# A hybrid block's planner gets new durations and handovers, and the attention copy is queued behind its scores

## The chip, the cores and the metric

The kernel runs on one core of one Trainium2 chip. The metric is the device time of one execution in microseconds (us), and lower is better. Times of before are the median of three runs.

## The reference

Two layers, each a mixer with three branches followed by a convolutional feed-forward network, on 16 meta tokens and 256 tokens of width 1024. All is float32. Cut to what matters:

```python
for li in range(DEPTH):                                   # DEPTH = 2
    h = h + mixer(rms_norm(h, norm_mix_g[li]), ...)
    h = h + conv_ffn(rms_norm(h, norm_ffn_g[li]), ...)
h = rms_norm(h, norm_final_g)
return h[:, PAD:]

def mixer(hn, ...):
    proj = hn @ w_in                                      # 1024 x 13312, split in 12
    o_ret = retention(rq, rk, rv, rg)                     # 4 heads, chunks of 128, decayed state
    o_hg = hgrn2(hq, hf, hi, hg, lb)                      # 8 heads, a gated scan: a = sum q k exp(cumsum gap)
    o_da = diff_attention(dq, dk, dv, lam, subln_g)       # 8 heads, two softmaxes subtracted, causal
    y = sum(sigmoid(gate_n) * (branch_n @ w_branch_n))
    return y @ w_out

def conv_ffn(hn, ...):
    u = hn @ w_ffn_in                                     # 1024 x 5632
    c = conv_b + sum(conv_w[j] * shifted(u, j) for j in range(3))
    return (silu(gate) * val) @ w_ffn_out                 # 2816 x 1024
```

## The kernel before

Activations are kept transposed, features on the partitions and the 272 tokens (16 meta + 256) in the free dimension; in the second layer most stages work on 258 or 256 tokens. TensorE has no full float32 product at this speed, so each factor is split into a high and a low part and each tile of 128 x 128 weights is multiplied three times: high by high (L923), low activations by high weights (L924), high activations by low weights (L925). In the profile these are the groups `main<-xh,whi`, `main<-xl,whi` and `main<-xh,wlo`: the "main matmuls". A triple of them is one step of the plan, recorded by `products` (L900 on).

All weights are one stream of some 400 chunks of 128 x 1024 (eight tiles). SyncE's queue loads a chunk into `wraw` (three buffers), ScalarE rounds it into `whi` (an activation that copies), VectorE subtracts and leaves `wlo`; `whi` and `wlo` have four buffers each. Twenty-four main matmuls use a chunk, in about 3 us.

Between the main matmuls stand the "side groups" of the three branches. Their names in the profile:

- `ms` is the matmul with ones that makes a norm's mean square, from `sum`; `rstd` follows on ScalarE, then the products `y<-h,rstd` on GpSimd.
- HGRN2 works in blocks: a group of small matmuls recorded by one helper (L1132: `lev`, `pm`, `far`), then VectorE's masked copies (`near<-masks,lev`, `am<-masks,pm`: a copy under a mask of bytes) and products (`hq`, `hf` with `tot`), ScalarE's copies into `at`, then `px` (whose copy is `ax`), `ht`, and the outputs `ho`. There are four such blocks, two in each layer. Each begins near 97, 197, 746 and 837 us.
- Retention: scores `s`, decayed on VectorE into `wts`, outputs `ro`, then a norm whose sums are reduced over the partitions by GpSimd (`hr<-sum`).
- Attention works on pairs of heads in `da_heads` (L1387 on): one step `scores` of the plan makes both heads' scores (`ds`), VectorE and ScalarE make the softmaxes in `two_a` and `two_b`, `wt` transposes them, ScalarE copies them into a buffer with the tag `wts` (the variable `a1`, "a head's weight buffer"; two of them), and `do` multiplies by the values. The first 16 columns of `a1`, for the meta tokens, are copied by GpSimd (`wts<-am`) from weights made earlier.

What sets the order of all this is written out by a planner. Every operation goes through `_Engine.__getattr__` (L601 is its recording line, which is why so many groups have that line), which gives it a duration by a formula of its size, and `_Plan.add`, which finds the operations on which it depends. Then `_Plan.order` runs a list scheduler over the whole program: at each step it takes the engine that can start first, and on it the operation with the smallest start, then the smallest key. The key is a due time (`plan.key`, `clock`); with the durations it decides the order. Constants in it:

- CROSS: the time from the end of an operation to the start of one on another engine that depends on it.
- FREE: the time from the last use of a buffer until another may take it.
- SWITCH: a change of ScalarE's activation table, 1.3.
- SHARED: the share by which a VectorE operation is taken to last longer while GpSimd is busy.
- PIECE, MANY, BEGIN: a group of 200 or more TensorE instructions may only begin in certain windows of each 256 instructions.

The plan fixes no time on the chip: it gives each engine its list of instructions, and the waits there are the semaphores of the data. The engines are recorded with the formulas `fixed + each * n`, n being the elements of a partition:

```python
act = _Engine(plan, nc.scalar, "act", 0.094, 0.833e-3)
dve = _Engine(plan, nc.vector, "dve", 0.068, 1.042e-3)
pool = _Engine(plan, nc.gpsimd, "pool", 0.04, 0.85e-3)
```

`plan.queue(first, last)` makes `first` wait for `last` in the plan; `plan.hold` lists buffers that an operation takes when it starts. PSUM is used as two buffers "main" of two banks, two "bank" and two "acc".

## Time and profile before

| | |
|---|---|
| median of 3 runs | 1285.73 us (1285.28 to 1286.61) |
| the profiled execution | 1286.2 us |
| its span | 1284.4 us |
| mean granted clock of TensorE | 0.999 |
| HBM read, written | 216.19 MB, 1.05 MB |
| DMA, mean | 175 GB/s |

The span is what the profiler records from the first to the last instruction; the profiled execution's own time is 1.8 us longer. A busy time of 99% for TensorE says that records lie end to end, and not that each is as short as it could be. The two layers lie one after the other: the matmul `ms` of the norm that opens the second starts at 665 us. A window of the profile is read as the busy time of each engine in a stretch; where TensorE has less than the length of the window, something was waited for there, and the timeline shows what.

The order of the instructions of both kernels is known without a run, as each program is built. TensorE has 10171 instructions in both, VectorE 1635, GpSimd 183, SyncE 445, and they are the same ones. ScalarE has six more table loads after the change (33 in place of 27). The orders differ from the first norm on; the first 99 main matmuls and the last stage have the same order. The largest moves on TensorE: the fourth HGRN2 block from 837.2 to 851.5 (in TensorE time, main matmuls and groups laid end to end with the lengths of before), the retention groups behind it some 9 us later, attention groups of the first layer 2 to 10 us earlier.

### The profile page before, as it was taken

The numbers are of one execution on the slowest core, as the hardware profiler recorded it, in microseconds if no ns is written. First come the engines' busy times: TensorE is split into PE (matmuls) and PEld (weight loads), VectorE is DVE, ScalarE is ACT, GpSimd is POOL, SyncE is SP. The second block draws the span as 40 slices with busy tenths as digits, with TensorE's granted clock in tenths as the row PEclk, the third lists the DMA queues.
The fourth block names the chain that finished last, engine by engine and source line by source line (L and its number), as shares of the span: only waits on it lengthen the run. The fifth ranks groups of instructions, "written<-read, shape, count | busy, mean of one in ns | idle before, by whom it ended". The sixth has DMA issues, their size and how long they took to land.

```text
span 1284.4 us, 26932 instructions
## 1 busy us (share of the span) xinstructions
PE 1275.5 (99%) x10825; PEld 1253.6 (98%) x10825; DVE 973.0 (76%) x1657; ACT 855.6 (67%) x1460; POOL 165.9 (13%) x174
## 2 busy tenths in 40 slices
PE   9999999999999999999999999999999999999998
PEld 9999999999999999999999999999999999999986
DVE  7686787698685789886565858886987867998753
ACT  6766575856776568776456754858567765787743
POOL 4001101132122020000020011012131210300000
PEclk9999999999999999999999999999999999999999
DMA  8655575544745555555555556745447466566663
GB/s 281 193 165 170 175 192 177 150 148 133 211 134 165 185 163 187 175 177 176 173 177 185 164 178 177 206 163 164 148 136 210 137 201 191 166 192 199 197 188 107
DMA packets 86093, 225.28 MB, mean 175 GB/s; under 512 B 32208, under 2 KB 32336, under 8 KB 85968
## 3 DMA queue, kind: packets, MB, share of 16 engines
q1 hardware_dynamic: 85680, 223.03, 56.9%
q8 instruction: 85, 1.39, 0.5%
q10 hardware_dynamic: 288, 0.52, 0.1%
q14 instruction: 40, 0.33, 0.1%
HBM read 216.19 MB, written 1.05 MB: 169 GB/s over the span
## 4 chain that ended last, share of the span: by engine, by line
PE 98%; DVE 1%; ACT 1%; DMA 0%; issue 0%; SPq 0%
PE main L925 29%; PE main L923 29%; PE main L924 28%; PE fo L1538 2%; PE fo L1540 2%; PE fo L1539 2%; PE ds L1409 1%; PE ro L601 1%; PE do L601 1%; PE ho L601 1%; PE lev L1132 1%; PE wt L601 0%; PE s L601 0%; DMA h<-in_h 0%; PE far L1132 0%; PE px L601 0%
## 5 line engine op out<-in xcount | busy, mean ns | idle before, releaser
L923 PE MATMUL main<-xh,whi 128*128 128x272 f32 (+1 forms) x2368 | 685.6, 290 | 0.2 <-ACT whi L601 0.2
L925 PE MATMUL main<-xh,wlo 128*128 128x272 f32 (+1 forms) x2368 | 679.6, 287 | 0.5 <-DVE wlo L601 0.4
L924 PE MATMUL main<-xl,whi 128*128 128x272 f32 (+1 forms) x2368 | 670.1, 283 | 0.0
L601 DVE TENSOR_TENSOR wlo<-wraw,whi 128x1024 fp32r<-128x1024 f32 (+1 forms) x408 | 507.1, 1249 | 205.6 <-ACT whi L601 203.3
L601 ACT ACTIVATE whi<-wraw 128x1024 fp32r<-128x1024 f32 (+1 forms) x408 | 426.2, 1049 | 211.8 <-PE main L924 118.7
L924 PEld LDWEIGHTS main<-xl,whi 128*128 128x128 f32 x2368 | 449.3, 190 | 0.3
L923 PEld LDWEIGHTS main<-xh,whi 128*128 128x128 f32 x2368 | 445.2, 188 | 1.7 <-ACT whi L601 0.4
L925 PEld LDWEIGHTS main<-xh,wlo 128*128 128x128 f32 x2368 | 444.5, 188 | 1.4 <-DVE wlo L601 1.4
L601 POOL PARTITION_ALL_REDUCE hr<-hsq x36 | 75.5, 2119 | 147.6 <-ACT hsq L601 147.5
L601 POOL TENSOR_TENSOR y<-h,rstd 128x272 f32<-128x272 f32 x32 | 38.5, 1235 | 319.6 <-ACT rstd L601 319.6
L601 DVE SCALAR_TENSOR_TENSOR two_b<-u,small,two_b 128x256 f32<-128x256 f32 (+2 forms) x176 | 78.4, 486 | 0.6 <-ACT two_b L601 0.2
L925 PE MATMUL main<-ghi,wlo 128*128 128x272 f32 x176 | 51.0, 290 | 0.0
L923 PE MATMUL main<-ghi,whi 128*128 128x272 f32 x176 | 50.8, 288 | 0.0
L924 PE MATMUL main<-glo,whi 128*128 128x272 f32 x176 | 50.1, 285 | 0.0
L601 ACT ACTIVATE two_b<-u,small 128x272 f32<-128x272 f32 (+1 forms) x88 | 49.4, 599 | 1.1 <-DVE glo L601 0.7
L601 ACT ACTIVATE u<-main 128x544 f32<-128x544 f32 (+1 forms) x40 | 24.5, 613 | 34.1 <-PE main L925 34.0
L923 PE MATMUL main<-b0hi,whi 128*128 128x272 f32 (+1 forms) x128 | 37.5, 293 | 0.0
L923 PE MATMUL main<-b1hi,whi 128*128 128x272 f32 (+1 forms) x128 | 37.3, 292 | 0.0
L925 PE MATMUL main<-yhi,wlo 128*128 128x272 f32 (+1 forms) x128 | 36.5, 285 | 0.0
L925 PE MATMUL main<-b2hi,wlo 128*128 128x272 f32 (+1 forms) x128 | 36.5, 285 | 0.0
L925 PE MATMUL main<-b1hi,wlo 128*128 128x272 f32 (+1 forms) x128 | 36.5, 285 | 0.0
L925 PE MATMUL main<-b0hi,wlo 128*128 128x272 f32 (+1 forms) x128 | 36.5, 285 | 0.0
(262 smaller groups left out, 1919.9 us busy)
## 6 DMA issues: line engine op xcount, KB each, us to landing
wraw<-in_w SPq DMA_DIRECT2D x402, 512.0 KB, 3.7
h<-in_h SPq DMA_DIRECT2D x4, 272.0 KB, 5.4
dec<-in_dec SPq DMA_DIRECT2D x2, 544.0 KB, 5.1
wraw<-in_w SPq DMA_DIRECT2D x4, 256.0 KB, 5.0
const<-in_const SPq DMA_DIRECT2D x1, 937.0 KB, 6.5
gain<-in_gl SPq DMA_DIRECT2D x1, 512.0 KB, 5.4
out<-y ACTq DMA_DIRECT2D x2, 256.0 KB, 2.7
out<-y SPq DMA_DIRECT2D x2, 256.0 KB, 2.6
```

The source lines that it names most:

```text
L601: self.plan.add(self.name, lambda: f(*args, **kw), cost, outs, ins, args[2] if method == "activation" else None, count)
L923: nc.tensor.matmul(o, wh, hi, start=first, stop=False)
L924: nc.tensor.matmul(o, wh, lo, start=False, stop=False)
L925: nc.tensor.matmul(o, wl, hi, start=False, stop=last)
L1132: nc.tensor.matmul(o, keys, x, start=True, stop=True)
L1409: nc.tensor.matmul(ss[m][:, at : at + nk], q[half, hd, q0 : q0 + P], k[half, hd, :nk], start=True, stop=True)
L1538: nc.tensor.matmul(o, gh, wh, start=False, stop=False)
L1539: nc.tensor.matmul(o, gl, wh, start=False, stop=False)
L1540: nc.tensor.matmul(o, gh, wl, start=False, stop=end)
```

## The change

The planner's model is changed in these places, and one dependency is added.

- Handovers: CROSS goes from 0.4 to 0.15 and a table LAG gives other values to some pairs of engines (0.35 into TensorE, 0.22 out of it to ScalarE or VectorE, 0 from TensorE to itself, 0 from SyncE's queue). FREE goes from 0.5 to 0.3.
- SHARED goes from 0.45 to 0.35 and counts only operations of VectorE that read two tensors from SBUF, against GpSimd's operations other than fills and copies.
- Durations: a reduction over the partitions of 272 columns from 1.87 to 2.10 us; a GpSimd product of 272 from 0.71 to 1.21; a GpSimd copy 0.3 more in place of 1.6e-3 for each element; a transpose from 0.11 to 0.08; a main triple of 272 from 0.349 to 0.374; the calls of an HGRN2 group from 0.034 to 0.03 each; a triple of 512 in the last stage from 0.676 to 0.693; a plain float32 matmul by 2400/2312.
- Sets of dependencies and of tiles become dictionaries, so that their order is that of insertion.
- `to_tokens` writes the same four copies and one transposing transfer in other words.
- In `da_heads` the two copies into the first columns of `a1` are recorded behind `scores` and queued behind it, so that each `a1` is taken with the scores.

```diff
@@ -330,17 +329,18 @@
 
     def __init__(self, engine, run, cost, key, func, count):
         self.engine, self.run, self.cost, self.key, self.func, self.count = engine, run, cost, key, func, count
-        self.tiles, self.need, self.after, self.ready = set(), 0, [], 0.0
+        self.tiles, self.need, self.after, self.ready = {}, 0, [], 0.0
 
 
 class _Plan:
 
 
 
-    CROSS = 0.4
-    FREE = 0.5
+    CROSS = 0.15
+    LAG = {("act", "pe"): 0.35, ("dve", "pe"): 0.35, ("pool", "pe"): 0.35, ("pe", "act"): 0.22, ("pe", "dve"): 0.22, ("pe", "pe"): 0.0, ("sp", "act"): 0.0, ("sp", "dve"): 0.0}
+    FREE = 0.3
     SWITCH = 1.3
-    SHARED = 0.45
+    SHARED = 0.35
 
 
 
@@ -381,23 +381,23 @@
 
     def add(self, engine, run, cost, outs, ins, func=None, count=0):
         op = _Op(engine, run, cost, self.key, func, count)
-        deps = set()
+        deps = {}
         for aps, write in ((ins, False), (outs, True)):
             for ap in aps:
                 n, lo, hi = self._span(ap)
                 if n not in self.seen:
                     continue
-                op.tiles.add(n)
+                op.tiles[n] = True
                 keep = []
                 for e in self.seen[n]:
                     if e[0] < hi and lo < e[1] and (write or e[3]):
-                        deps.add(e[2])
+                        deps[e[2]] = True
                         if write and lo <= e[0] and e[1] <= hi:
                             continue
                     keep.append(e)
                 keep.append((lo, hi, op, write))
                 self.seen[n] = keep
-        deps.discard(op)
+        deps.pop(op, None)
         op.need = len(deps)
         for d in deps:
             d.after.append(op)
@@ -409,7 +409,7 @@
     def hold(self, *tiles):
 
         for t in tiles:
-            self.ops[-1].tiles.add(t.tensor.name)
+            self.ops[-1].tiles[t.tensor.name] = True
 
     def queue(self, first, last):
 
@@ -485,7 +485,7 @@
 
         self.end = engines
         self.busy = {e: 0.0 for e in engines}
-        taken = 0.0
+        taken = shared = 0.0
 
         def comes(op):
             return op.count < self.MANY or (int(taken) - self.BEGIN.start) % self.PIECE < len(self.BEGIN)
@@ -516,9 +516,9 @@
                 continue
             now[e].remove((c, op))
             cost = op.cost
-            if e == "dve" and engines["pool"] > t:
-
-                cost += min(engines["pool"] - t, self.SHARED * cost)
+            if op.func == "both" and shared > t:
+
+                cost += min(shared - t, self.SHARED * cost)
             if op.func in self.SETS and self.SETS[op.func] != tables:
                 tables = self.SETS[op.func]
                 cost += self.SWITCH
@@ -531,6 +531,8 @@
                     f = free[self.tag[n]]
                     f.remove(min(f))
             engines[e] = t + cost
+            if op.func == "shared":
+                shared = t + cost
             self.busy[e] += cost
             taken += op.count * (1 + self.SEMS)
             done = t + cost + (2.0 if e == "sp" else 0.0)
@@ -540,7 +542,7 @@
                     free[self.tag[n]].append(done + self.FREE)
             for o in op.after:
                 o.need -= 1
-                o.ready = max(o.ready, done + (self.CROSS if o.engine != e else 0.0))
+                o.ready = max(o.ready, done + self.LAG.get((e, o.engine), self.CROSS))
                 if o.need == 0:
                     push(o)
             if op.run is not None:
@@ -565,6 +567,15 @@
     def __init__(self, plan, engine, name, fixed, each):
         self.plan, self.engine, self.name, self.fixed, self.each = plan, engine, name, fixed, each
 
+    def _kind(self, method, args, ins):
+
+        if method == "activation":
+            return args[2]
+        if self.name == "pool" and method not in ("memset", "tensor_copy"):
+            return "shared"
+        if method in ("tensor_tensor", "scalar_tensor_tensor") and not any(x.tensor.name in self.plan.psum for x in ins):
+            return "both"
+
     def __getattr__(self, method):
         f = getattr(self.engine, method)
 
@@ -574,12 +585,16 @@
             ins = [x for k, x in aps if k not in (0, "out", "accum_out")]
             n = math.prod(outs[0].shape[1:])
             cost = self.fixed + self.each * n
+            if self.name == "act" and ins[0].dtype == U16 and ins[0].tensor.name not in self.plan.psum:
+                cost += 0.33e-3 * n
             if self.name == "act":
                 cost += 0.093 * (len(aps) - 2) - (0.043 if ins[0].tensor.name in self.plan.psum else 0.0)
             elif method == "partition_all_reduce":
-                cost = 0.4 + 5.4e-3 * n
+                cost = 0.5 + 5.9e-3 * n
+            elif self.name == "pool" and method == "tensor_copy":
+                cost += 0.3
             elif self.name == "pool" and method != "memset":
-                cost += 1.6e-3 * n
+                cost += 0.75 + 0.7e-3 * n
             if method == "scalar_tensor_tensor":
                 cost += 0.06
             if method == "reciprocal":
@@ -587,18 +602,18 @@
             elif method == "tensor_tensor_scan":
                 cost += self.each * n
             elif method == "transpose":
-                cost = 0.11
+                cost = 0.08
             elif method == "matmul" and args[1].dtype == F32R:
-                cost = max(0.107, n / 2400 + 0.003)
+                cost = max(0.107, 0.458e-3 * n)
             elif method == "matmul":
-                cost = max(0.214 if args[1].shape[-1] > 32 else 0.07, 4 * n / 2400)
+                cost = max(0.214 if args[1].shape[-1] > 32 else 0.07, 4 * n / 2312)
             elif method == "dma_start_transpose":
                 cost = 1.5
             elif method == "dma_start":
                 cost = self.fixed + self.each * n * outs[0].shape[0]
 
             count = self.name == "pe" and (2 if method == "transpose" or args[1].dtype == F32R else 4)
-            self.plan.add(self.name, lambda: f(*args, **kw), cost, outs, ins, args[2] if method == "activation" else None, count)
+            self.plan.add(self.name, lambda: f(*args, **kw), cost, outs, ins, self._kind(method, args, ins), count)
 
         return call
 
@@ -910,7 +925,7 @@
         if (name, j) == ("fo", 3):
 
             to[j, 1] = main()[:, 1, :]
-        cost = 3 * ((T - t0) / 2400 + 0.003)
+        cost = 3 * 0.458e-3 * (T - t0)
         left = dict.fromkeys(to, _ktiles(name))
         for _, i, k, f in tiles:
             hi, lo = (x[:, t0:] for x in xs(k))
@@ -956,24 +971,28 @@
         act.activation(hi, x, AF.Copy)
         tt(lo, x, hi.bitcast(F32), SUB)
 
-    def half_words(t):
-
-        return t.bitcast(U16).rearrange("p a (t h) -> p h a t", h=2)
+    def words(t):
+
+        return t.bitcast(U16).rearrange("p (t h) -> p h t", h=2)
+
+    def turn(to, src):
+
+        turned = to.rearrange("p (n x) -> p n x", x=P)
+        sync.dma_start_transpose(turned, src)
+        return turned.rearrange("p (h n) x -> p h n x", h=2)
 
     def to_tokens(ps, vt, e):
 
-        src = new(tp, [P, 2, 2, 2 * P], U16, "vsrc", 2, "vsrc")
-        words = half_words(ps[:, :, : 2 * P])
+        src = new(tp, [P, 8 * P], U16, "vsrc", 2, "vsrc")
+        parts = src.rearrange("p (h f t) -> p h f t", h=2, f=2)
         for h in range(2):
-            act.activation(src[:, h], words[:, h], AF.Copy)
+            act.activation(parts[:, h], ps[:, :, : 2 * P].bitcast(U16).rearrange("p f (t h) -> p h f t", h=2)[:, h], AF.Copy)
         plan.key += 1.0
-        turned = new(tp, [P, 8, P], U16, "vtr", 1, "vtr")
-        sync.dma_start_transpose(turned, src.rearrange("p h f t -> p (h f t)"))
+        turned = turn(new(tp, [P, 8 * P], U16, "vtr", 1, "vtr"), src)
         plan.key += 4.0
-        turned = turned.rearrange("p (h f c) x -> p h c f x", h=2, f=2)
-        to = half_words(vt[:, :, e : e + 2 * P])
+        to = vt[:, :, e : e + 2 * P].bitcast(U16).rearrange("p c (f x h) -> p h c f x", h=2, f=2)
         for h in range(2):
-            act.activation(to[:, h].rearrange("p c (f x) -> p c f x", f=2), turned[:, h], AF.Copy)
+            act.activation(to[:, h], turned[:, h].rearrange("p (f c) x -> p c f x", f=2), AF.Copy)
 
     def tail_tokens(tails):
 
@@ -1131,7 +1150,7 @@
                     for o, keys, x in calls:
                         nc.tensor.matmul(o, keys, x, start=True, stop=True)
 
-                plan.add("pe", run, 0.034 * len(calls) + 0.1, outs, [*ins], count=4 * len(calls))
+                plan.add("pe", run, 0.03 * len(calls) + 0.1, outs, [*ins], count=4 * len(calls))
 
             lanes = [slice(t, t + 32) for t in range(0, P, 32)]
 
@@ -1397,8 +1416,6 @@
             for _ in heads:
                 red = temp(12, "dm")
                 stats.append([red[:, 4 * i : 4 * i + 4].rearrange("p (t m) -> p t m", m=2) for i in range(3)])
-            for a1, hd in zip(a1s, heads):
-                pool.tensor_copy(a1[:, :META], st[f"dw{b}"][:, hd * META : (hd + 1) * META])
 
 
             def scores():
@@ -1408,8 +1425,11 @@
                             half = slice(64 * m, 64 * m + 64)
                             nc.tensor.matmul(ss[m][:, at : at + nk], q[half, hd, q0 : q0 + P], k[half, hd, :nk], start=True, stop=True)
 
-            plan.add("pe", scores, 1.8, [x[:, : T + P + META] for ss in sss for x in ss], [q[:, heads[0] : heads[-1] + 1, :], k[:, heads[0] : heads[-1] + 1, :]], count=32)
+            got = plan.add("pe", scores, 1.8, [x[:, : T + P + META] for ss in sss for x in ss], [q[:, heads[0] : heads[-1] + 1, :], k[:, heads[0] : heads[-1] + 1, :]], count=32)
             plan.hold(*sum(sbs, []), *a1s)
+            for a1, hd in zip(a1s, heads):
+                pool.tensor_copy(a1[:, :META], st[f"dw{b}"][:, hd * META : (hd + 1) * META])
+                plan.queue(plan.ops[-1], got)
             for ss, sb, (nm, _, _) in zip(sss, sbs, stats):
                 for i, (q0, nk, at) in enumerate(tiles):
                     mask = const[:, C_MASK + T - nk : C_MASK + T]
@@ -1519,7 +1539,7 @@
             for t in range(2):
                 for k in range(KD):
                     pe.matmul(accs[t][k // 4][:, k % 4 * P : (k % 4 + 1) * P], h[:, k, tokens(t)], ident, is_transpose=True, start=k % 4 == 0, stop=False)
-            cost = 3 * (BANK / 2400 + 0.012)
+            cost = 3 * 0.231
             groups = [(t, c) for t in range(2) for c in range(2)]
             chunks = {}
             order = [(k, t, c) for k in range(FK - LATE) for t, c in groups]
```

## The prediction

> **What bounds the kernel now.** I read the page first (busy time, slices, chain), then the waits of TensorE, then windows of 20 us, then the timeline where a window is not full.
>
> ```profile
> PE 1275.5 (99%) x10825; PEld 1253.6 (98%) x10825; DVE 973.0 (76%) x1657; ACT 855.6 (67%) x1460; POOL 165.9 (13%) x174
> PEclk9999999999999999999999999999999999999999
> PE 98%; DVE 1%; ACT 1%; DMA 0%; issue 0%; SPq 0%
> ```
>
> TensorE is busy for 1275.5 of 1284.4 us at full granted clock, and the chain that ended last is 98% TensorE. A change of order alone can move the end only through TensorE's waits, its first microseconds and its tail. So the question is how long TensorE waits now, and where it will wait after.
>
> ```profile
> PE warm L601 <- POOL ones_d L601: 1.0, 1, 1.0
> PE ro L601 <- DVE wts L601: 0.5, 1, 0.5
> PE px L601 <- DVE near L601: 0.5, 1, 0.5
> PE main L925 <- DVE wlo L601: 0.4, 2, 0.2
> PE ro L601 <- DVE at L601: 0.3, 1, 0.3
> PE main L923 <- ACT whi L601: 0.2, 1, 0.2
> ```
>
> ```profile
> 0.00:20.00 20.00, 18.27 (x121) 17.08 (x122) 12.36 (x17) 14.26 (x23) 5.56 (x11) 1.00 0.78 265
> 200.00:220.00 20.00, 19.74 (x152) 19.15 (x151) 16.21 (x34) 12.53 (x22) 2.37 (x2) 1.00 0.46 151
> 740.00:760.00 20.00, 19.42 (x287) 18.87 (x286) 12.59 (x24) 11.07 (x18) 1.01 (x1) 1.00 0.55 167
> 840.00:860.00 20.00, 19.54 (x157) 19.03 (x156) 17.50 (x38) 11.89 (x22) 2.42 (x3) 1.00 0.43 136
> 480.00:500.00 20.00, 20.00 (x163) 20.00 (x161) 19.93 (x40) 15.50 (x26) 0.00 (x0) 1.00 0.54 163
> ```
>
> Each wait row is total, times, longest; each window row is the length, then busy time of PE, PEld, DVE, ACT and POOL, then clock and DMA. The list of waits is complete and adds up to 2.9 us, and besides the first 20 us (1.73 idle) only three of the windows that I read were short: 0.26, 0.58 and 0.46 us. The last row is a stretch in which VectorE is full and TensorE still loses nothing. The three short windows are the retention and HGRN2 blocks.
>
> Their waits are a little longer than "idle" says, because a matmul record is longer than its pitch. I therefore read starts:
>
> ```profile
> 210.30 0.29 PE L925 MATMUL main<-xh,wlo 128*128 128x272 f32 x1
> 210.85 0.97 PE L601 MATMUL ro<-wts,rvt 128*128 128x272 f32 x4 [0.26 <-DVE at L601]
> 751.07 0.28 PE L925 MATMUL main<-xh,wlo 128*128 128x258 f32 x1
> 751.48 0.76 PE L601 MATMUL px<-hq,hf 128*128 128x144 f32 x4
> 751.98 0.38 PE L923 MATMUL main<-xh,whi 128*128 128x258 f32 x1
> 752.19 0.28 PE L924 MATMUL main<-xl,whi 128*128 128x258 f32 x1
> 752.31 0.28 PE L925 MATMUL main<-xh,wlo 128*128 128x258 f32 x1
> 753.05 0.73 PE L601 MATMUL px<-hq,hf 128*128 128x144 f32 x4 [0.46 <-DVE near L601]
> 849.19 0.28 PE L925 MATMUL main<-xh,wlo 128*128 128x258 f32 x1
> 849.93 0.95 PE L601 MATMUL ro<-wts,rvt 128*128 128x258 f32 x4 [0.46 <-DVE wts L601]
> ```
>
> The pitch of the main matmuls is 0.12 us (752.19 to 752.31). What lies beyond it in front of a side group is the wait: 210.30 to 210.85 gives 0.43, 751.07 to 751.48 gives 0.29, 752.31 to 753.05 gives 0.62, 849.19 to 849.93 gives 0.62. Together 1.96 us in mid-run. The Trainium skill (Perfetto Trace Analysis, "Tensor Engine Instruction (MATMUL, LD_WEIGHTS)") says that the end of a TensorE record is estimated, not observed; by recorded ends alone the mid-run sum would be 1.30 us, the three windows, and I keep 1.96.
>
> **The change part by part.** No instruction of TensorE, VectorE, GpSimd or SyncE is added or removed; ScalarE gets six more table loads. Everything else is order: the plan's durations, handovers (CROSS, LAG, FREE, SHARED) and one dependency. Sets that became dictionaries, and the re-expressed token transposes, issue the same instructions: 0.
>
> *Corrected matmul costs.* A main triple of 272 columns goes from 0.349 to 0.374 us in the plan. This does not make TensorE faster, it only lets other engines be planned less hurriedly: 0 by itself. Of the first 99 main matmuls and of the work after the last block the order is unchanged (the load of the final gain goes one weight transfer later on SyncE's queue, 0: the gain is used only in the tail, which keeps its time), so most of the 1.73 us of the start stays.
>
> *The first norm.*
>
> ```profile
> 16.95 2.13 POOL L601 TENSOR_TENSOR sum<-sum,two_c 128x544 f32<-128x544 f32 x1 [2.07 <-ACT two_c L601]
> 19.11 0.44 DVE L601 TENSOR_TENSOR sum<-sum 128x272 f32<-128x272 f32 x1 [1.25 <-POOL sum L601]
> 20.07 0.62 PE L601 MATMUL ms<-sum,ones_d 128*128 128x272 f32 x2
> ```
>
> The `ms` matmul moves six main matmuls forward, 6 x 0.125 = 0.75 us, from 20.07 to 19.32. Its input is complete at 19.11 + 0.44 = 19.55, because GpSimd's sum ends at 19.08. This is a new wait of 0.2 to 0.4 us (without and with a handover of 0.14, which 751.45 + 1.46 to 753.05 below shows); I take +0.3. Behind it on TensorE stand the main matmuls.
>
> *Third HGRN2 block (747 to 755).*
>
> ```profile
> 748.90 1.20 DVE L601 COPY_PREDICATED am<-masks,pm 64x64 f32<-64x64 uint8 x5
> 750.01 0.88 DVE L601 TENSOR_TENSOR hf<-hf,tot 128x256 f32<-128x256 f32 x2
> 750.80 0.62 DVE L601 TENSOR_TENSOR hq<-hq,tot 128x448 f32<-128x448 f32 x1
> 751.45 1.46 DVE L601 COPY_PREDICATED near<-masks,lev 128x192 f32<-128x192 uint8 x4
> ```
>
> VectorE now makes five masked copies, two `hf`, one `hq` from 748.90 to 751.42, then `px` starts at 751.48. After the change the order is am, hf, am, hq, am, hf: two masked copies fewer ahead of `px`, 2 x 0.24 = 0.48 us, so `px` is ready at about 751.0. But it stands nine main matmuls earlier on TensorE: 751.48 - 0.29 - 9 x 0.12 = 750.1. Wait 0.9 us; if the interleaving also hides the gap that each dependent pair leaves, 0.6. The second `px` used to wait for `near` (ends 752.91) and now lands in another PSUM bank: no wait. So 0.29 + 0.62 becomes 0.6 to 0.9: -0.3 to 0, I take -0.05.
>
> *Second block and its retention group (200 to 212).* The `ro` that waits 0.43 now keeps its place. Bounds: gone (-0.43), or its wait joined by one as large as the largest row, 0.62. I take 0, since VectorE's order before it is hardly altered.
>
> *Fourth block.* It moves 14.4 us later on TensorE, behind two more retention scores; `ro` follows 7.6 us later than now. Between the block and its first `px` stand 21 main matmuls, 2.5 us; VectorE needs 1.46 + 0.88 + 0.62 = 2.96 us by the rows above, but can begin with `lev`, ahead of the block's far part. So `px` waits 0 to 0.6. The old wait of `ro` for `wts` goes (-0.62), for the masks that delay `wts` now stand behind it. I take +0.2 for `px`: -0.4; high end two waits of 0.62, +0.62.
>
> *First block, norms, attention pairs.* No wait shows there now. `ho` of the first block is taken some 4 us earlier and `ms` of the later norms 1.4 to 3.9 us earlier, so one new wait of the size seen elsewhere (0.3 to 0.6) may appear: 0 to +0.6, I take +0.3.
>
> *The copy in the attention heads.*
>
> ```profile
> L601 POOL COPY wts<-am 128x16 f32<-128x16 f32 x16 | 8.6, 554 | 64.4 <-ACT am L601 59.1 <-PE do L601 5.3
> L601 POOL PARTITION_ALL_REDUCE hr<-hsq x36 | 75.5, 2119 | 147.6 <-ACT hsq L601 147.5
> L601 POOL TENSOR_TENSOR y<-h,rstd 128x272 f32<-128x272 f32 x32 | 38.5, 1235 | 319.6 <-ACT rstd L601 319.6
> ```
>
> Sixteen copies of 0.55 us now stand behind their pair's scores, some behind the next reduction (2.12 us). Covered by the softmax between scores and output, and by a GpSimd that is busy 13%: 0. Without that cover the next thing late would be the pair's `do` matmul, 0.55 us for each of eight pairs, 4.4 us. A buffer taken later can only free TensorE's scores to go earlier, which is what the order shows (attention groups 2 to 10 us earlier); the main matmuls behind them were not waiting, so nothing is gained.
>
> *Six more table loads.*
>
> ```profile
> L601 ACT ACT_TABLE_LOAD x14 | 18.0, 1283 | 1.8 <-DVE two_b L601 1.5
> L557 ACT ACT_TABLE_LOAD x13 | 16.7, 1283 | 0.9 <-PEq L1733 0.7
> ACT whi L601 <- PE main L924: 118.7, 92, 3.7
> DVE wlo L601 <- ACT whi L601: 203.3, 187, 4.7
> SPq L601 <- DVE wlo L601: 785.7, 304, 8.5
> ```
>
> 6 x 1.283 = 7.7 us of ScalarE, which waits 118.7 us in total for TensorE to release a weight buffer: the loads lie under those waits, 0. All six stand at gates and norms of the retention and HGRN2 stages, one at a time; exposed they would cost the 7.7.
>
> **Sum.** +0.3 - 0.05 + 0 - 0.4 + 0.3 = +0.15. Low ends: 0.2 - 0.3 - 0.43 - 0.62 + 0 = -1.15. High ends: 0.4 + 0 + 0.62 + 0.62 + 0.6 = +2.2. The profiled execution took 1286.2 us (span 1284.4 and 1.8 around it), which would become 1286.35; it lies 0.5 above the median of the three runs, 1285.73. From the median: 1285.9, own range 1284.6 to 1287.9.
>
> **The rivals.**
>
> *A, the waits go.* If the plan now knows the true durations, the 1.96 us vanish and no new wait comes: 1283.8; with the start's 1.73 too, at most 3.7 us, 1282.0. For it: three of the four waits lie in the blocks whose order changes. Against: the first norm is put ahead of its input by my own rows.
>
> *B, slower: margins cut, masks still too cheap.*
>
> ```profile
> L601 DVE COPY_PREDICATED near<-masks,lev 128x128 f32<-128x128 uint8 x16 | 6.0, 376 | 0.5
> L601 DVE COPY_PREDICATED am<-masks,pm 64x32 f32<-64x32 uint8 x16 | 3.4, 210 | 0.6
> L601 DVE COPY_PREDICATED near<-masks,lev 128x192 f32<-128x192 uint8 x8 | 3.3, 409 | 0.8 <-PE lev L1132 0.6
> L601 DVE COPY_PREDICATED near<-masks,lev 128x64 f32<-128x64 uint8 x8 | 2.1, 264 | 0.3
> L601 DVE COPY_PREDICATED am<-masks,pm 64x64 f32<-64x64 uint8 x4 | 0.9, 219 | 0.5 <-PE pm L1132 0.5
> ```
>
> The plan still prices a VectorE operation at 0.068 + 1.042e-3 n us, so these masked copies (n = 128, 32, 192, 64, 64) cost it 3.2 + 1.6 + 2.1 + 1.1 + 0.5 = 8.6 us; they take 15.7. Half of the `near` and all of the `am` stand late in a block: (11.4 - 6.4) / 2 + (4.3 - 2.2) = 4.6 us, 1.15 a block. The handovers PE to VectorE, VectorE to ScalarE and VectorE to PE lose 0.18 + 0.25 + 0.05 = 0.48 of margin. If TensorE's group stands exactly where the plan believes it ready, each block costs 1.63 us. Four blocks: 6.5 - 1.96 + 0.3 = +4.9, 1290.6; three: +3.2, 1288.9; two: +1.6, no difference. So it decides from three blocks on. Against it: in the second and fourth block I count slack.
>
> *C, weights late.* Table loads and earlier side work delay the weight halves in full stretches. All six loads exposed: 1293.4; two of them 1288.3. Against: the waits above, 203.3 us of VectorE for ScalarE included, and the full window at 480.
>
> *D, GpSimd in VectorE's way.*
>
> ```profile
> 22.66 3.41 DVE L601 TENSOR_TENSOR wlo<-wraw,whi 128x1024 fp32r<-128x1024 f32 x2 [0.22 <-ACT whi L601]
> 36.03 2.35 DVE L601 TENSOR_TENSOR wlo<-wraw,whi 128x1024 fp32r<-128x1024 f32 x2
> ```
>
> Two subtracts beside GpSimd's products take 3.41 us, two alone 2.35: 0.53 more each, where the new plan charges 35% of 1.14, 0.40. With 44 reductions and 32 products, 76 meetings by 0.13 are 10 us of VectorE that the plan does not see; all exposed, 1295.6. Against: the old plan's 0.51 was near the truth, but VectorE has 24% idle and TensorE lost nothing in those stretches. The Trainium skill (SBUF: State Buffer, "Who interferes with whom") says that whichever of the two starts first keeps the shared port for its whole instruction; by it a subtract could lose a whole reduction, and the rows above show a smaller loss than that.
>
> *E, the plan does not do what it says,* and the order moves nothing that binds: 1285.7.
>
> **How the numbers follow.** My forecast 45% (no difference), A 15% (about half of it beyond 0.2%), B 27%, of which 25 beyond 0.2%, C 6%, D 3%, E 4%. About 0.2%, 2.6 us, is what a measurement of this kernel can tell from no change. Faster: 8%. Slower: 25 + 6 + 3 = 34%. The rest, 58%, within. Range: down to 1283.3, where a half of A still lies, and up to 1290.2, most of B; C, D and the ends of A and B stay out, under 2 in 10.
>
> **What would show it.** TensorE's waits name `ms` once, at 19.3 us, 0.2 to 0.4: the norm's step. One `px` wait near 750 of 0.6 to 0.9 and none at the second: the third block. No `ro` wait for `wts` near 858: the fourth. Six more table loads with ScalarE's wait for TensorE smaller by about 8 us: cover right. Wrong if the main matmuls wait for `whi` or `wlo` by more than 1 us in sum (C, D), if three blocks show waits over 1.5 us (B), or if TensorE's waits in mid-run are under 0.5 us (A).

## The result and the profile after

The changed kernel takes 1289.47 us (median of 7 runs, 1288.52 to 1290.23) against 1285.28 (median of 7, 1284.99 to 1286.61). The ratio is 1.0029, 95% interval 1.0018 to 1.0041: slower by 0.3%, 4.2 us. The forecast was 1285.9 with no difference as the likeliest case, the range 1283.3 to 1290.2, and slower a chance of 0.34.

The page of the changed kernel, first section, and its chain:

```profile
PE 1276.2 (99%) x10825; PEld 1253.6 (97%) x10825; DVE 960.5 (75%) x1657; ACT 862.8 (67%) x1466; POOL 169.4 (13%) x174
PE 40%; DVE 0%; ACT 0%; issue 0%
```

Nothing of this explains 4 us: the same matmuls, 7 us more of ScalarE for the six table loads, a VectorE that is a little less busy. The chain is followed back only part of the way. The waits of TensorE say more (columns as before: total, times, longest):

```profile
PE wt L616 <- POOL dt L616: 1.4, 2, 0.8
PE warm L616 <- POOL ones_d L616: 1.0, 1, 1.0
PE main L938 <- ACT whi L616: 0.6, 1, 0.6
PE ho L616 <- ACT at L616: 0.5, 1, 0.5
PE ho L616 <- DVE ho L616: 0.4, 1, 0.4
PE main L940 <- DVE wlo L616: 0.4, 2, 0.2
PE ro L616 <- DVE at L616: 0.2, 1, 0.2
```

The waits of `px` and of `ro` for `wts` are gone. New are two of `wt` for `dt`, the largest item, and two of `ho`. (The 0.6 for `whi` stands at 5.9 us, where both kernels still have the same order, and costs nothing against the trace of before.) `dt` is the buffer in which GpSimd collects the last 16 columns of each head's attention weights (the tails); one transpose for each four heads turns them on TensorE, so there are four such transposes in the kernel. The windows of the same kernel show where (length, PE, PEld, DVE, ACT, POOL):

```profile
300.00:320.00 20.00, 19.22 (x156) 18.63 (x153) 17.14 (x47) 11.98 (x37) 6.79 (x7) 1.00 0.38 128
380.00:400.00 20.00, 19.38 (x152) 18.69 (x151) 15.04 (x29) 14.67 (x37) 8.27 (x9) 1.00 0.42 137
740.00:760.00 20.00, 20.00 (x296) 19.84 (x295) 11.67 (x25) 10.19 (x18) 1.01 (x1) 1.00 0.52 159
840.00:860.00 20.00, 20.00 (x291) 19.67 (x290) 15.97 (x35) 9.37 (x16) 1.01 (x1) 1.00 0.49 155
```

The HGRN2 windows are full now, and two attention windows are short. The timeline of the first of them, TensorE's, then GpSimd's, then VectorE's:

```profile
309.88 0.29 PE L940 MATMUL main<-xh,wlo 128*128 128x272 f32 x1
310.94 0.33 PE L616 MATMUL wt<-const,dt 128*128 128x128 f32 x1 [0.78 <-POOL dt L616]
```
```profile
306.40 0.48 POOL L616 COPY dt<-two_a 128x16 f32<-128x16 f32 x2 [8.66 <-DVE two_a L616]
308.21 2.68 POOL L616 COPY dt<-two_a 128x16 f32<-128x16 f32 x2 [1.34 <-DVE two_a L616]
```
```profile
308.34 2.36 DVE L616 TENSOR_TENSOR wlo<-wraw,whi 128x1024 fp32r<-128x1024 f32 x2
```

Two copies of 16 columns take 0.48 us at 306.40 and 2.68 at 308.21. The second pair begins 0.13 us ahead of two subtracts of VectorE (its first copy alone lasts 2.54) and is done when they are done: 308.34 + 2.36 = 310.70, 308.21 + 2.68 = 310.89. The transpose behind it starts at 310.94, 0.94 us later than the pitch of 0.12 allows after 309.88. At 386.65 the same happens.

How much each place costs is read by the lag: the start of the same main matmul in two traces, taken only where the same instructions lie ahead of it in both. Against the second profile of the kernel before (1284.92 us, span 1283.1; why that one follows below), the first profile of the changed kernel (span 1286.8):

```
place (us)   lag after it   step   what waits there
  20            0.39        0.39   ms of the first norm
 104            0.59        0.20   px of the first HGRN2 block
 211            0.47       -0.12   ro waits a little less
 257            1.13        0.66   ho, for VectorE's ho
 311            2.15        1.02   wt for dt
 387            3.25        1.10   wt for dt, and do around it
 764            3.94        0.69   ho, for ScalarE's at
 850 to 909     3.39       -0.55   ro no longer waits for wts
 924 to 1217    3.70        0.31   attention of the second layer
```

3.70 is the difference of the spans. In a second profile of the changed kernel (1289.38 us) the lag ends at 4.43: 0.3 more before 20 us, a further step of 0.5 at 36 us, and 0.4 in place of 0.66 at 257.

### The profile page after: what moved, and what is told of

It reads as the page before. It is cut to its first block, busy times and chain, and to the rows that moved or that the text cites. A ratio compares the mean times of both kernels' runs of the same rounds, so it can differ in the third digit from the quotient of the medians.

```text
span 1286.8 us, 26929 instructions
## 1 busy us (share of the span) xinstructions
PE 1276.2 (99%) x10825; PEld 1253.6 (97%) x10825; DVE 960.5 (75%) x1657; ACT 862.8 (67%) x1466; POOL 169.4 (13%) x174
## 5 line engine op out<-in xcount | busy, mean ns | idle before, releaser
L616 ACT ACTIVATE whi<-wraw 128x1024 fp32r<-128x1024 f32 (+1 forms) x408 | 427.6, 1050 | 203.2 <-PE main L939 144.9
L616 POOL PARTITION_ALL_REDUCE hr<-hsq x36 | 72.7, 2046 | 136.8 <-ACT hsq L616 130.8
```

Source lines behind the costliest of these rows:

```text
L616: self.plan.add(self.name, lambda: f(*args, **kw), cost, outs, ins, self._kind(method, args, ins), count)
```

## The experiments

Theory T: the loss is a handful of side groups that the new plan sets ahead of their inputs, above all the two tail transposes, whose copies on GpSimd are held by VectorE. Rivals: many small losses from the shorter handovers (M); the durations rather than the handovers (P); the moved copy alone (C); execution-to-execution differences at the start (X). All times are medians; the changed kernel stands at 1289.2 to 1289.5, the kernel before at 1285.2 to 1285.7.

**The copies on ScalarE.** Order kept, engine changed:

```diff
 pool.tensor_copy(st[f"dt{b}"][:, g, hd, :], w[:, c : c + TAIL])
+to, src = st[f"dt{b}"][:, g, hd, :], w[:, c : c + TAIL]
+plan.ops[-1].run = lambda to=to, src=src: nc.scalar.activation(to, src, AF.Copy)
```

> The changed kernel, every engine's order kept, but the 32 copies of attention tails into dt run on ScalarE at the same place of the plan instead of GpSimd. Theory T (a dt copy on GpSimd is held by two subtracts of VectorE for 2.54 us, and the transpose of the tails waits on TensorE for it): both waits of wt for dt go, the lag against the kernel before no longer rises by 1.1 us at 310 and by 1.1 at 387, and the time falls by about 2.2 us to 1287.3. Rival M (the plan's shorter handovers put the transposes too near to the softmax itself, whoever copies): waits of 0.3 or more remain at both places, 1288.5 or more. Rival S (ScalarE is the tighter engine): its 32 copies of 0.2 us delay the weight halves and the time stays at 1289.5 or rises.

Measured: 1288.09 (11 runs), ratio to before 1.0019 [1.0010, 1.0028]. TensorE's timeline of this kernel at the first place:

```profile
310.45 0.29 PE L940 MATMUL main<-xh,wlo 128*128 128x272 f32 x1
310.57 0.27 PE L616 MATMUL wt<-const,dt 128*128 128x128 f32 x1
```

0.12 us, the bare pitch: no wait, and `wt` is gone from its list of waits. The 32 copies in the view of the tile `dt`, of the kernel before and of the changed one (shortest, median and longest, ns, then first and last start), and on ScalarE in this kernel's groups (busy, mean ns):

```profile
L601 POOL COPY dt<-two_a x32: 197/198/1131, 291.5 to 1024.1; 128x16 f32<-128x16 f32 x32
```
```profile
L616 POOL COPY dt<-two_a x32: 191/271/2543, 287.7 to 1024.0; 128x16 f32<-128x16 f32 x32
```
```profile
L1464 ACT ACTIVATE dt<-two_a 128x16 f32<-128x16 f32 x32 | 5.9, 204 | 0.1
```

On GpSimd the same copy takes 0.2 us or up to 2.54; on ScalarE all take 0.2.

So the wait is GpSimd's copy held by VectorE, as T says: the order of TensorE is the same, and the input of the copies (`two_a`) was there in time. The gain, 1.3 us, is less than the 2.2 expected: in the trace the step at 311 is gone whole, but 0.4 of the one at 387 stays, and 0.4 is lost at 36 us, where a main matmul waits for `xl`.

**The transposes later.** A helper takes a group out of TensorE's finished order and sets it n weight tiles later, with what depends on it in between on other engines:

```diff
+MOVES = [("dt_242_", 6), ("dt_325_", 6)]
 order = [None] + self.order()
+for name, n in MOVES:
+    order = self.later(order, name, n)
```

> The changed kernel, but in the first layer the two transposes of the tails (and VectorE's product behind each) stand six weight tiles (18 main matmuls, 2.25 us) later; nothing else moves. Theory T: the wait was 1.1 us at each place, so both go and nothing takes their place: about 1287.3. Rival M (many small misplacements, of which these are the visible ones): the tails' users, do from tw, become late in turn and at least half of the 2.2 us stays: 1288.4 or more.

Measured: 1287.41 (11 runs), 1.0017 [1.0008, 1.0026]. 2 us won, as expected; both steps are gone but for 0.2. Taking the group 2 us later cost nothing that the trace shows behind it.

**The duration alone.** In place of moves by hand, the plan is told what a held copy costs:

```diff
 pool.tensor_copy(st[f"dt{b}"][:, g, hd, :], w[:, c : c + TAIL])
+plan.ops[-1].cost = 1.25
```

> The changed kernel, but the plan charges each copy of the tails into dt 1.25 us, what it takes when a subtract of VectorE holds it, in place of 0.35; the plan then sets the tail transposes later by itself. Theory T: the two waits of 1.1 us go, 1289.4 - 2.2 = 1287.2, as when they were set later by hand (1287.4). Rival R (each plan is a new draw): other waits come in, 1288.2 or more.

Measured: 1287.54 (11 runs), 1.0015 [1.0006, 1.0023]: the same 2 us. Both waits of `wt` are gone, and the other waits stay where they were. For these two waits one duration is enough: 0.35 in place of 1.25, which lies between the 1.13 and 1.41 us of copies that one subtract held. It is not what made them new, though: the formula of before charged the same copy even less, 0.04 + 2.45e-3 x 16 = 0.08 us, and had no such wait.

**All new waits (five_late).**

```diff
+MOVES = [("ms_31_", 2), ("ho_224_", 6), ("dt_242_", 6), ("dt_325_", 6), ("ho_540_", 6)]
```

> The changed kernel, with all five places at which its trace shows a new wait of TensorE set later: ms of the first norm by two tiles (its place of before), ho at 257 and at 764 and both tail transposes by six tiles, with what depends on them. Theory T in its full form (the whole loss is a handful of side groups taken before their inputs, 0.2 + 0.65 + 1.1 + 1.1 + 0.75 = 3.8 us, and the gains at the third and fourth HGRN2 block, 1.07 and 0.6, stand by themselves): 1289.5 - 3.8 = 1285.7. Rival M: each group that is set later makes its own users late, so less than half is won back: 1287.6 or more.

Measured: 1286.38 (11 runs), 1.0009 [1.0000, 1.0018]: 3.0 won of the 3.8 expected. The five waits are gone, but two others stand in the list:

```profile
PE warm L637 <- POOL ones_d L637: 1.0, 1, 1.0
PE lev L1172 <- DVE extra L637: 0.7, 1, 0.7
PE main L961 <- DVE wlo L637: 0.6, 3, 0.2
PE main L960 <- DVE xl L637: 0.5, 1, 0.5
```

`lev` of the fourth block (823 us) had been covered: a TensorE that arrives earlier (by 1.9 us in this profile) finds VectorE's chain not ready. That much of M is right.

**Two and three more moves.** `lev` six tiles later, and GpSimd's `hq` of the first norm behind seven `y` again (seven_moves); then also two subtracts behind the fifth `xl` (eight_moves):

```diff
-MOVES = [("ms_31_", 2), ("ho_224_", 6), ("dt_242_", 6), ("dt_325_", 6), ("ho_540_", 6)]
+MOVES = [("ms_31_", 2), ("ho_224_", 6), ("dt_242_", 6), ("dt_325_", 6), ("ho_540_", 6), ("lev_600_", 6)]
+order = self.hq_back(order)
+order = self.swap(order, "wlo10_", "xl1_")
+order = self.swap(order, "wlo9_", "xl1_")
```

> The changed kernel with the five groups set later as in five_late, and two more: lev of the fourth block by six tiles (it waited 0.72 for VectorE's extra in five_late), and GpSimd's product hq of the first norm behind seven of the products y in place of four, as it stood before the change. Theory T+X: five_late's 1286.4 less 0.7 (lev) and less 0.7 (xl waits near 36) is 1285.0, a little below the kernel before. Rival M (each removed wait appears at the next group, since VectorE's chains are what is late): no better than five_late, 1286.2 or more.

> seven_moves, and in the first norm VectorE makes the fifth xl ahead of two subtracts, as before the change, instead of behind them. Theory X (main matmuls wait up to 0.7 us at 36 us for that xl, since two subtracts beside GpSimd's products take 3.5 to 4.1 us): that wait goes, 1286.6 - 0.7 = 1285.9, and no other moves. Rival M: the same lateness comes out at the next weight halves (wlo), 1286.4 or more.

Measured: 1286.56 (11 runs), 1.0007 [0.9998, 1.0015], and 1286.02 (11 runs), 1.0003 [0.9994, 1.0012]. In seven_moves the wait of `lev` went, 0.8 us by the lag, yet the median did not fall. In eight_moves the time is as expected but for the wrong reason: the fifth `xl` is early now, but a main matmul waits for a later one, and the 0.9 us won at the first are lost again at the second. That is rival M's mechanism, at `xl` and not at `wlo`:

```profile
36.01 0.40 PE L987 MATMUL main<-xl,whi 128*128 128x272 f32 x1 [0.66 <-DVE xl L664]
```

VectorE still makes two subtracts ahead of the last three `xl`, where the kernel before makes one. Whether that order brings the wait was not tried, and stays open.

**The copy in the attention heads alone (copy_alone)**, in the kernel before with its old plan:

> The kernel before, with its old durations and handovers, and only the edit in the attention heads: the copies into the first columns of the weight buffers are queued behind the pair's scores. Theory T (the loss comes from the new durations and handovers): no difference, 1285.3, within 0.6. Rival C (the copy's new place is what makes the attention stretches late): 1287 or more, with waits of wt or do for GpSimd.

Measured: 1285.68 (11 runs), 1.0004 [0.9995, 1.0013]: no difference is seen, within -0.6 to +1.7 us, and neither `wt` nor `do` waits for GpSimd.

**The halves of the new plan**, with the copies behind the scores in both. First the old handovers; then the old durations and SHARED, all of them, with the new handovers:

```diff
-CROSS = 0.15
+CROSS = 0.4
-FREE = 0.3
+FREE = 0.5
-o.ready = max(o.ready, done + self.LAG.get((e, o.engine), self.CROSS))
+o.ready = max(o.ready, done + (self.CROSS if o.engine != e else 0.0))
```

> The changed kernel, but CROSS 0.4, FREE 0.5 and no LAG, as before; the new durations and the copies behind the scores stay. Theory H (the shorter handovers lose the 4 us: groups are taken as soon as the plan believes their inputs there): 1286.3 or less, with at most one wait of wt for dt. Rival P (the new durations do): 1288.5 or more. Rival R (each plan is a new draw, and falls anywhere between 1284 and 1290 by which few groups happen to stand too early): the waits stand at other groups than those of the changed kernel.

> The changed kernel, but all durations and SHARED as before; the new handovers and the copies behind the scores stay. Theory H: most of the loss stays, 1288.5 or more. Rival P: 1286.3 or less. Rival R: waits at other groups than those of the changed kernel, with a time that follows from their sum.

Measured: 1288.0 (11 runs, 1287.15 to 1290.97), 1.0021 [1.0013, 1.0030], and 1287.64 (11 runs), 1.0015 [1.0006, 1.0024]. Each half alone loses rather more than half of it, 2.3 to 2.6 us, and at different places. The first waits with the old handovers (in a profiled execution 3 us above its median, so only their places count), and with the old durations:

```profile
PE ro L616 <- DVE wts L616: 1.5, 1, 1.5
PE ro L616 <- DVE at L616: 1.1, 1, 1.1
PE main L939 <- DVE xl L616: 1.1, 1, 1.1
```
```profile
PE main L936 <- DVE wlo L612: 1.5, 2, 1.3
PE wt L612 <- POOL dt L612: 1.4, 2, 1.0
```

This is rival R: each plan is a new draw of which groups stand too early. The wait for `dt` stands in the profiles with the new handovers, whichever durations, and not in the one with the old; the rest of the loss does not belong to a half. Which single constant puts which group too early was not traced.

**Each kernel again**, for a second profile:

> The changed kernel once more, as it is. Its profiled execution was 0.85 us under the median of its seven runs. Theory X (the stretch 22 to 36 us, where GpSimd's products of the first norm and VectorE's xl and wlo hold each other, differs from execution to execution): the median stays at 1289.2 to 1289.7, and this profile shows up to 0.5 us of waits of main matmuls for xl near 36 us that the first one did not have. Rival (the profiled executions are simply other ones at random over the whole span): the lag against the kernel before differs in steps all over.

> The kernel before, as it is, for a second profile: its first profiled execution, 1286.2 us, was 0.8 over the median of all runs of it. Theory X (the first 40 us differ from execution to execution, the rest of the span does not): a profile near 1285.4 lies 0.5 to 0.9 us ahead of the first one already at 40 us and keeps that lead to the end, and the four waits of mid-run stand as they were. Rival: the lead is gathered at the mid-run waits, which are then shorter.

Measured: 1289.22 (7 runs) and 1285.20 (11 runs). The changed kernel's second profile has the same places and one more, of 0.5 at 36 us, where a main matmul waits for `xl` (theory X):

```profile
36.15 0.39 PE L939 MATMUL main<-xl,whi 128*128 128x272 f32 x1 [0.23 <-DVE xl L616]
```

Of the kernel before, the second profile ends 1.3 us ahead of the first, and here the rival was right: the lead is not made in the first 40 us (0.2) but at `px` in the third block. TensorE's timeline of the second profile, against 0.29 and 0.62 of wait in the first:

```profile
750.83 0.28 PE L925 MATMUL main<-xh,wlo 128*128 128x258 f32 x1
750.95 0.65 PE L601 MATMUL px<-hq,hf 128*128 128x144 f32 x4
...
751.67 0.28 PE L925 MATMUL main<-xh,wlo 128*128 128x258 f32 x1
751.79 0.71 PE L601 MATMUL px<-hq,hf 128*128 128x144 f32 x4
```

Both gaps are the pitch of 0.12. So 0.9 us of the waits on which the prediction stood is not in every execution. Where it came from shows on ScalarE, whose `whi` ahead of this block waits for a weight transfer, first in the first profile, then in the second:

```profile
746.66 1.06 ACT L601 ACTIVATE whi<-wraw 128x1024 fp32r<-128x1024 f32 x1 [1.98 <-DMA wraw<-in_w]
```
```profile
745.39 1.06 ACT L601 ACTIVATE whi<-wraw 128x1024 fp32r<-128x1024 f32 x1 [0.70 <-DMA wraw<-in_w]
```

That transfer landed 6.6 us after its issue in the one and 5.6 in the other. Behind it VectorE's subtract, and with it the masked copies that `px` needs, begin 1.3 us later (748.90 against 747.63). Two more profiles have the same order of work here: in copy_alone the transfer took 6.8 us and `px` waits, in the last kernel below it took 5.5 and `px` does not. Why it sometimes takes longer stays open.

**A version that beats both.** The kernel before, with its plan, and the two waits of `ro` that both its profiles show taken away:

```diff
+MOVES = [("ro_165_", 4), ("ro_623_", 6)]
```

> The kernel before, with its own plan, but the two retention outputs at which TensorE waits in every profile of it (ro at 211, 0.43 us, ro at 850, 0.62 us) set later by four and by six weight tiles. Theory T (a side group taken before its input costs its wait and nothing else, so it is won back by taking it later): both waits go, 1285.4 - 1.0 = 1284.4, the shortest of all kernels here. Rival M (the lateness of VectorE's chain comes out at the next group or at the weight halves): 1285.2 or more, with a wait at another ro or at wlo.

Measured: 1284.24 (11 runs, 1283.62 to 1285.21), against 1285.54 (15 runs): 0.9990 [0.9981, 0.9999]. TensorE's whole list of waits is then

```profile
PE warm L622 <- POOL ones_d L622: 1.0, 1, 1.0
PE main L946 <- DVE wlo L622: 0.2, 1, 0.2
PE main L944 <- ACT whi L622: 0.2, 1, 0.2
```

and the 1.0 us expected was won (1.3 by the medians, 0.1 to 2.4 by the interval, which only just leaves out no change; 1.1 by the lag against the second profile of before).

## Why the prediction was right or wrong

*The bound and its price were right*: TensorE, with the change worth only what its waits become. But the time lies above the sum's own range (1284.6 to 1287.9). It is inside the wider one, 1283.3 to 1290.2, whose upper part was there for rival B, and B's mechanism did not occur: that the range held is in part luck. The likeliest case was not what happened.

*The copy in the attention heads: right as it stood, and the wrong copies.* The moved `wts` copies cost nothing (copy_alone). But the prediction priced those 16 and passed over the 32 `dt` copies beside them in the same function, whose user is a TensorE group. Their row in the trace of before already had 198 ns as the median and 1131 as the longest.

*First block, norms, attention pairs, 0 to +0.6: the step that failed.* It allowed one new wait there. The runs showed five: 0.2 at 104, 0.66 at 257, 1.02 at 311, 1.1 at 387, 0.3 in the second layer, 3.3 us, of which 2.1 is the tail transposes. "(attention groups 2 to 10 us earlier); the main matmuls behind them were not waiting, so nothing is gained" was true and not the point: an earlier group can lose.

*The first norm, +0.3*: right, 0.39 between the two profiles, though the list of waits does not name `ms` as the prediction said it would: the matmul ahead of it is recorded to 19.30 us, and `ms` starts at 19.42. Setting it back wins the 0.4 at 20 us in five_late's trace; that this shortens the whole was not shown, because of the waits for `xl` behind it.

*The third block, -0.05: a wrong ready time and a missed wait.* `px` was to wait 0.6 to 0.9 after the change and waits not at all. VectorE's timeline after:

```profile
751.04 0.42 DVE L616 TENSOR_TENSOR hf<-hf,tot 128x256 f32<-128x256 f32 x1 [0.59 <-PE far L1151]
751.49 0.23 DVE L616 COPY_PREDICATED am<-masks,pm 64x32 f32<-64x32 uint8 x1
751.60 0.61 DVE L616 TENSOR_TENSOR hq<-hq,tot 128x448 f32<-128x448 f32 x1
752.14 0.23 DVE L616 COPY_PREDICATED am<-masks,pm 64x32 f32<-64x32 uint8 x1
752.24 0.42 DVE L616 TENSOR_TENSOR hf<-hf,tot 128x256 f32<-128x256 f32 x1
```

VectorE sits idle 0.59 us until the far part is there, and is done with the second `hf` at 752.66; `px` starts at 753.13. The prediction counted from 748.90, where VectorE began in the first profile, late by the transfer told of above; in the second profile it began at 747.63. A masked copy put between two products also delays the next one by 0.11 (751.49 to 751.60), not by 0.24, which the low end allowed for. Against the second profile of before, where `px` does not wait either, nothing was gained. And `ho` of this block waits 0.69 at 764, which the prediction had not looked at.

*The second block, 0*: right within 0.12 (by starts `ro` waits 0.33, in the two profiles of before 0.43 and 0.45). *The fourth block, -0.4*: nearly right, -0.55, as `px`, taken at +0.2, does not wait.

*The table loads, 0*: right, ScalarE's idle time ahead of `whi` fell from 211.8 to 203.2 us, 8.6, near the 7.7 of the loads. But the sign that the prediction named, a smaller wait for TensorE, was the wrong row: that wait rose, from 118.7 to 144.9. What fell is ScalarE's wait for weight transfers, 43.0 and 44.8 us in the two profiles of before, 7.4 and 12.4 in those of after.

*Rival B came out in sign and nearly in size, and not by its mechanism.* It wanted three HGRN2 blocks to wait for masked copies; `px` waits in none over 0.2. *Rival D had the right resource and the wrong side*: it let GpSimd hold VectorE's subtracts. Here VectorE holds GpSimd's copies, for up to 2.54 us, where a free copy takes 0.20. The Trainium skill (SBUF: State Buffer, "Who interferes with whom") says that of the two the one that starts second is blocked until the other's instruction is over. The trace agrees where a copy starts 0.14 us after a subtract and ends 0.05 us after it (360.50, in the last section); the holds of 2.54 us last over more than one instruction.

The new plan with the copies ahead of the scores was not tried on the chip and could not be: there the planner finds no order at all, as two waiting copies hold both weight buffers.

## What to carry to other kernels

An operation that is either free or blocked (0.20 or 1.1 to 2.5 us here) has no single duration that a list scheduler can use: 0.35 lies between the two and fits neither. Give it the blocked one, or set its user later. Where the bound engine is full, a side group taken too early costs its whole wait, and one taken 2 us later cost nothing as long as it was not itself waited for. So waits are removed one by one in a plan that is nearly right (1.0 us by two moves) rather than by a new plan, with a look after each move at what the earlier TensorE now finds not ready (`lev`, `xl`). And take two profiles of the kernel before: of 1.96 us of waits in the first, 0.9 came with one late weight transfer and were gone in the second.

## What the runs showed of the hardware

How long VectorE holds a GpSimd copy of 16 columns depends on where the copy starts. In the thirteen profiles with these copies on GpSimd, every one that starts up to 0.15 us into a subtract is let go when that subtract ends (1.13 to 1.23 us), and in twelve of these cases another subtract followed without a pause. From the second profile of before, VectorE, then GpSimd:

```profile
360.36 2.35 DVE L601 TENSOR_TENSOR wlo<-wraw,whi 128x1024 fp32r<-128x1024 f32 x2
```
```profile
360.50 1.13 POOL L601 COPY dt<-two_a 128x16 f32<-128x16 f32 x1 [0.41 <-DVE two_a L601]
```

One that starts inside the `two_a` product just ahead of two subtracts, as the second pair above does, lasted until the second of them ended in 25 of 28 cases (2.54 us), and until the first ended in the other three (1.41). What decides between these, the traces do not show.

The same weight transfer landed 5.6 and 6.6 us after its issue in two executions of the kernel before, and `px` waited behind the later one; the two spans differ by 1.3 us, both at a clock of 0.999.
